# A one-core encoder layer: order of the Gram products, place of the decay's tanh, place of the inverse's products, and order of the first down tile

## The chip, the cores and the metric

The kernel runs on one core of one Trainium2 chip. The metric is the device time of one execution in microseconds (us), the median of several runs. A core has a matrix engine (TensorE, in the profile PE, with PEld for its weight loads), VectorE (DVE), ScalarE (ACT), GpSimd (POOL) and a queue engine (SyncE, SP) that here issues all DMAs. Each engine works through its own list of instructions in a fixed order, and waits on semaphores for the others. SBUF is the on-chip memory, PSUM the small memory into which TensorE writes.

## The reference

One layer of a streaming encoder: sequence 1024, width 1024, batch 1, all in float32. Three groups of heads (64 wide) work side by side: mLSTM (4 heads), retention (6), RWKV-7 (6). Then comes a SwiGLU feed-forward of width 2816 and a last RMSNorm.

```python
h = rmsnorm(x, ln1_g)
pm, pr, pw = split(h @ w_in)
y = concat(mlstm_group(pm), retention_group(pr), rwkv7_group(pw))
x = x + y @ w_out
h = rmsnorm(x, ln2_g)
x = x + (silu(h @ w_gate) * (h @ w_up)) @ w_down
out = rmsnorm(x, lnf_g)
```

The part of RWKV-7 that matters here:

```python
w_log = -softplus(-(w0 + tanh(wl) @ w_up)) - 0.5
decay = exp(-exp(w_log))                     # equals exp(-exp(-0.5) * sigmoid(w0 + ...))
kk = k * k_k, normalised per head;  k = k * (1 + (a - 1) * k_a)
S = S * w_t - (S kk_t)(kk_t * a_t)^T + v_t k_t^T ;  y_t = S r_t      # per frame
```

## The kernel before, in words

**Number form.** Large matrix products are made of three products: each float32 operand is split into a rounded high part (`split_hi`, line 90, ScalarE) and the remainder (`split_lo`, line 93, VectorE), and high x high, high x low and low x high are summed in PSUM. `three` (lines 119 to 121) does it for the projections, lines 740 to 742 for the products laid out by token, `product` (1218 to 1220) for gate and up, `mult` in `down` (1412 to 1414) for down. Their weights come through `w_part` (line 101). These are called dense work below. The mixers' small matmuls take float32 operands directly.

**How the order comes about.** The mixers' work is written as Python generators. `weave` runs them against a planned clock: a generator yields `(cost, delay)`, the clock advances by the cost, and it is called again once the delay is over, or yields the name of an event that another generator signals. `rwkv_proj`, `fillers` and `out_proj` share the dense work, a quarter of a tile at a time (`PART`, 1.38 us). The tile framework then orders each engine's instructions with a scheduler of its own: earlier written goes first, but what it foresees as ready may pass what is not. `tc.issue_after(ins)` forbids this for what is written inside it on the engine of `ins`: it stays behind `ins` in the queue, without waiting for its end. `weave` uses it to keep a generator's TensorE instructions behind the last dense one.

**RWKV-7.** Heads go in three pairs (`i`), the sequence in two halves (`h`), so there are six half-sequences, each of eight chunks of 64 frames. Head `q` (0 even, 1 odd) of a pair lies on partitions `rows_of(q)`, 0 to 63 or 64 to 127. Of one half-sequence:

- `rwkv_half` prepares it. `pa` (line 391) and `pw` (393) are the projections of the rates; `th` (395) is the tanh of the first. Then come `kk` (397), its squares (399), their sums (402), the new keys, the bonus `pb` (412), and the centred values `pt` (421) with their four copies (423 to 426). `cs` (428) is the tanh of the decay, from `pw`; 429 to 431 turn it into running sums, and `er` (434) and `ek` are exponentials of them. Lines 456 to 459 build `kb` and `E`.
- The Gram matrices follow (line 466): for each group of four chunks (`c0`), two PSUM tiles, one for each head; VectorE masks them into `E` (472 to 474). The loop is written chunk by chunk with the two heads in turn, but nothing holds the scheduler to it.
- `rwkv_inverse` solves the unit triangular systems. Their blocks go to DRAM (`ab_d`) and come back rearranged (`MN`, `R`), VectorE solves them (520 to 528), the result goes out (`r_d`, 534) and back into `E` (538). VectorE transposes two blocks (542); TensorE makes the off-diagonal blocks by two sets of 16 small products (547 and 553), with ScalarE copies between (550, 556).
- `rwkv_chain` carries the state through the chunks (588 to 618). It waits for the inverse. The preparation of pair `i`, half `h` begins when the chain of pair `i - 1`, half `h` is done. `rwkv_out` (655) takes the results.

PSUM tiles come from three rings: `acc` (3 buffers), `misc` (3) and `chain` (2). All of the mixers' small products but the chain's use `misc`. Most float32 temporaries of the preparation come from a ring of nine (`tmp`, tag `t`).

**Feed-forward.** `wino` makes gate and up for pairs of 128-row tiles from 7 products each for gate and up (5 for the first pair), items in a list in order. `down(h, d, sl)` makes one output tile from 22 row tiles `f` in six items of up to four (`f0` = 0, 4, ..., 20); an item's weights are prepared three items ahead (`AHEAD`). Its operands are the activations of half `h`: they were stored to `a_dram`, are fetched back by `fetch` into the two `rg` buffers (line 1356), and split by `take`; those of `f` 18 to 21 (`DIRECT`) of the first half are still in SBUF and not fetched. `GROUPS` are `f` 0 to 7, 8 to 15 and 16 to 21. Which `take` comes after which item is written out at the end:

```python
if i == last - 9:
    fetch(0, 0)
if i in (last - 5, last - 4):
    take(0, i - last + 5)
elif i in (last - 1, last + 1):
    take(0, 2, slice((i - last + 1) // 2, (i - last + 1) // 2 + 1))
```

`last` is the index of the first down item. So `f` 0 to 7 are taken at `last - 5`, 8 to 15 at `last - 4`, 16 to 19 at `last - 1`, 20 and 21 at `last + 1`.

Of the kernel before, what the change touches and what calls it, by code (L numbers as in the profile page):

```python
# [11 lines left out]
F32 = mybir.dt.float32  # L12
F32R = mybir.dt.float32r
AF = mybir.ActivationFunctionType
# [5 lines left out]
P = 128  # L20
T = 1024
D = 1024
HF = 512
# [4 lines left out]
FT = D_FF // P  # L28
# [26 lines left out]
def trunk_kernel(ctx: ExitStack, tc: tile.TileContext, a: dict, out: bass.AP):  # L55
# [16 lines left out]
    def misc_tile():  # L72
        return ps_m.tile([P, HF], F32, name="misc", tag="misc")
# [55 lines left out]
    def late(eng):  # L129

        return tc.issue_after(next(i for i in reversed(nc.cur_bb.bb.instructions) if i.engine == eng.engine))
    dense = [None]

    def signal(name, after=0.0):
        events[name] = clock[0] + after
# [40 lines left out]
    two = (0, 1)  # L176
# [12 lines left out]
    def rows_of(q):  # L189
        return slice(q * 64, (q + 1) * 64)  # L190
# [196 lines left out]
    def rwkv_half(i, h, r, k, v):  # L387
# [5 lines left out]
        PE.matmul(pw, lhsT=up[0:64, ch], rhs=wa[h][0:64, :], start=True, stop=True)  # L393
        th = tmp(name="th")
        S.activation(th, pa, AF.Tanh, scale=0.5, bias=ha0[:, i:i + 1])
        kk = tmp(name="kk")
        S.activation(kk, k, AF.Copy, scale=vc("k_k", i))
        t1 = tmp(name="t1")
# [25 lines left out]
        S.copy(out=X[0:64, 0::2, 1, :], in_=p4[0:64, :, 1, :])  # L424
        S.copy(out=X[64:128, 0::2, 0, :], in_=p4[0:64, :, 0, :])
        S.copy(out=X[0:64, 1::2, 1, :], in_=p4[64:128, :, 1, :])
        cs = tmp(name="cs")
        S.activation(cs, pw, AF.Tanh, scale=0.5, bias=hw0[:, i:i + 1])
        V.tensor_scalar(cs, cs, 0.5, 0.5, ALU.mult, ALU.add)
        for z in (slice(z, z + P) for z in range(0, HF, P)):  # L430
            V.tensor_tensor_scan(cs[:, z], data0=cc("reset"), data1=cs[:, z], initial=0.0, op0=ALU.mult, op1=ALU.add)
# [28 lines left out]
        yield 1.2, 7.0  # L460
        for c0 in range(0, 8, 4):
            grams = [misc_tile().rearrange("p (c x) -> p c x", c=4) for _ in two]
            for c in range(4):
                for q, g4 in enumerate(grams):
                    rows = rows_of(q)
                    PE.matmul(g4[:, c, :], lhsT=kb[rows, c0 + c, :, :].rearrange("p a t -> p (a t)"),
                              rhs=E[rows, c0 + c, q, 128:256], start=True, stop=True)
            for q, g4 in enumerate(grams):
                rows, orow = rows_of(q), rows_of(1 - q)
                cs4 = slice(c0, c0 + 4)  # L470
                msk = cc("mask_k").unsqueeze(1).broadcast_to([P, 4, 64])
                V.tensor_tensor(E[orow, cs4, q, 192:256], g4[rows, :, 0:64], msk[rows], ALU.mult)
                V.tensor_tensor(E[orow, cs4, q, 128:192], g4[orow, :, 0:64], msk[orow], ALU.mult)
                V.tensor_tensor(E[:, cs4, q, 64:128], g4[:, :, 64:128],
                                cc("mask_r").unsqueeze(1).broadcast_to([P, 4, 64]), ALU.mult)
# [30 lines left out]
    def rwkv_inverse():  # L506
        for i in range(3):
            for h in range(2):
                yield f"ab{i}{h}"
                E, ab_d = hv_E[i, h]  # L510
                MN = sb.tile([P, 32, 32], F32, name="MN", tag="MN")
                R = sb.tile([P, 8, 32], F32, name="R", tag="R")
                SY.dma_start(out=MN, in_=ab_d.rearrange("b q c s t -> (b q c) (s t)").unsqueeze(0).broadcast_to([4, 32, 1024]))
                SY.dma_start(out=R, in_=ab_d.rearrange("b q c (j g) t -> g (b q c) j t", g=4))
                yield 0.0, 11.0

                mf = MN.rearrange("p s t -> p (s t)")
                tv = ev.tile([P, 516], F32, name="rt", tag="ev")[:, 0:480].rearrange("p (s t) -> p s t", t=32)
                with late(V):
                    V.tensor_tensor(tv, mf[:, 34:34 + 15 * 66:66].unsqueeze(2).broadcast_to([P, 15, 32]), MN[:, 2:31:2], ALU.mult)  # L520
                V.tensor_tensor(MN[:, 1:30:2], MN[:, 1:30:2], tv, ALU.add)
                for u in range(1, 31, 2):
                    n, w = (u + 4) // 4, 31 - u
                    tv = sb.tile([P, 256], F32, name="rt", tag="tq", bufs=2)[:, 0:2 * n * w].rearrange("p (s j t) -> p s j t", j=2, t=w)
                    V.tensor_tensor(tv, R[:, 0:n, u:u + 2].unsqueeze(3).broadcast_to([P, n, 2, w]),
                                    MN[:, u:u + 2, u + 1:32].unsqueeze(1).broadcast_to([P, n, 2, w]), ALU.mult)
                    for j in range(2):
                        V.tensor_tensor(R[:, 0:n, u + 1:32], R[:, 0:n, u + 1:32], tv[:, :, j], ALU.add)
                yield 0.0, INV
                r_d = dram.tile([2, 2, 8, 32, 32], F32, name="r_d", tag=f"r_d{i}{h}")  # L530
                rf = R.rearrange("p s t -> p (s t)")
                for g in range(4):
                    G.memset(rf[lane(g), g::36], 1.0)
                SY.dma_start(out=r_d.rearrange("b q c (j g) t -> g (b q c) j t", g=4), in_=R)
                T11, Q = (sb.tile([P, 8, 32], F32, name="tq", tag="tq", bufs=2) for _ in two)
                for q in range(2):
                    for b in range(2):
                        SY.dma_start(out=E[blk(q, b), :, q, col(b)], in_=r_d[b, q].rearrange("c s t -> s c t"))
                yield 0.0, 9.0
                for q in range(2):  # L540
                    with late(V):
                        V.transpose(out=T11[blk(q, 0)], in_=E[blk(q, 0), :, q, col(0)])
                pqr = misc_tile()
                q3, r3 = (pqr[:, z:z + 256].rearrange("p (c t) -> p c t", c=8) for z in (0, 256))
                for c in range(8):
                    for q in range(2):
                        PE.matmul(q3[blk(q, 1), c, :], lhsT=E[blk(q, 0), c, q, col(1)], rhs=T11[blk(q, 0), c, :],
                                  start=True, stop=True)
                for q in range(2):
                    S.copy(out=Q[blk(q, 1)], in_=q3[blk(q, 1)])  # L550
                for c in range(8):
                    for q in range(2):
                        PE.matmul(r3[blk(q, 0), c, :], lhsT=Q[blk(q, 1), c, :], rhs=E[blk(q, 1), c, q, col(1)],
                                  start=True, stop=True)
                for q in range(2):
                    S.copy(out=E[blk(q, 0), :, q, col(1)], in_=r3[blk(q, 0)])
                signal(f"inv{i}{h}", 2.5)
                yield 1.7, 3.0
# [620 lines left out]
    with ExitStack() as ph3:  # L1179
# [221 lines left out]
        def down(h, d, sl):  # L1401
            box = {}

            def mult(f0, w):
# [27 lines left out]
                if d == KT - 1:  # L1432
# [2 lines left out]
                    ends[0] = final(h, sl, [sqa, sq])  # L1435

            return [(lambda f=f: w_split(w_part(a["w_down"][d][:, f:min(f + 4, FT)])), lambda w, f=f: mult(f, w))
                    for f in range(0, FT, 4)]

        ends = [iter(())]  # L1440
        pairs = [wino(j, m) for j in range(FT // 2) for m in two]
# [62 lines left out]
        for i in range(len(items) + AHEAD):  # L1504
# [6 lines left out]
            ready[i] = None  # L1511
            if i == last - 9:
                fetch(0, 0)
            if i in (last - 5, last - 4):
                take(0, i - last + 5)
            elif i in (last - 1, last + 1):
                take(0, 2, slice((i - last + 1) // 2, (i - last + 1) // 2 + 1))
            if i == last - 1:
                for h in two:
                    x3[h] = big.tile([P, KT, HF], F32, name="x3", tag="E")  # L1520
# [96 lines left out]
```

## Time and profile before

| what | value |
|---|---|
| median of 3 runs | 1493.16 us (1493.12 to 1493.8) |
| profiled execution: its own time | 1485.33 us |
| profiled execution: span from first to last instruction | 1483.5 us |
| mean granted TensorE clock | 0.969 |
| busy share: TensorE, VectorE, ScalarE, GpSimd | 95%, 60%, 37%, 29% |
| mixers and first half's output, 0 to 735 us | TensorE 682.91 us busy, clock 0.95 |
| gate and up, 800 to 1223 us | TensorE 422.92 us busy, clock 1.00 |
| first down tile, 1223 to 1240 us | TensorE 12.57 us busy, clock 0.90 |

Busy times are unions over an engine's instructions. The granted clock is what the chip's throttle allowed TensorE, as a share of full speed. A row of the timeline gives start, length (both us), engine, line and operation, output and inputs, count, and in brackets the idle time of the engine before it and what ended it. A row of windows gives start and end of the stretch, its length, the busy time of each engine with its number of instructions, the granted clock, and the share and rate of the DMA engines. A row under a line's own view names whom the engine waited for, the total in us and how many times. Float32 matmuls stand as two instructions each, and each has a weight load.

### The profile page before, as it was taken

How to read it: one execution, taken by the hardware profiler on the slowest of the kernel's cores; microseconds unless marked ns; L12 is line 12 of the kernel's file. 1: busy time of each engine (PE TensorE's matmuls, PEld its weight loads, DVE VectorE, ACT ScalarE, POOL GpSimd, SP SyncE). 2: the span in 40 equal slices, each digit the busy share in tenths (PEclk: the TensorE clock that was granted, in tenths of full speed). 3: DMA queues.
4: the chain of work that ended last, by engine and by line, in shares of the span. 5: the costliest groups of instructions: out<-in, count | busy, mean ns of one | idle time of the engine just before them, and what ended most of it. 6: DMA issues, size and time to landing. Idle time of an engine off the chain costs nothing.

```text
span 1483.5 us, 23145 instructions
## 1 busy us (share of the span) xinstructions
PE 1410.4 (95%) x8450; PEld 1145.0 (77%) x8450; DVE 890.6 (60%) x1760; ACT 545.2 (37%) x1179; POOL 436.5 (29%) x539
## 2 busy tenths in 40 slices
PE   7998998989999999999998999999999999999997
PEld 5777777887767888887776887888888877888886
DVE  7457585676766757755587555555555574347434
ACT  7352344323223243344545332233333354224222
POOL 3211022335433232334374444443333420000000
PEclk9998999979997999999999999999999999999998
DMA  5132232344431344463542222222222138337333
GB/s 203 51 132 66 67 98 77 81 116 125 126 85 56 100 123 141 121 196 109 178 160 72 76 86 86 85 86 85 86 86 79 52 137 285 97 96 240 98 97 117
DMA packets 131461, 165.33 MB, mean 111 GB/s; under 512 B 44532, under 2 KB 80532, under 8 KB 130196
## 3 DMA queue, kind: packets, MB, share of 16 engines
q1 hardware_dynamic: 131348, 163.87, 34.9%
q8 instruction: 66, 1.08, 0.3%
q14 instruction: 47, 0.39, 0.1%
HBM read 126.06 MB, written 37.77 MB: 110 GB/s over the span
## 4 chain that ended last, share of the span: by engine, by line
PE 70%; DVE 7%; DMA 5%; issue 5%; ACT 3%; POOL 3%; SPq 1%; DVEq 0%; POOLq 0%; ACTq 0%
PE acc L1218 5%; PE acc L1219 5%; PE acc L1220 5%; PE chain L1414 5%; PE chain L1413 5%; PE chain L1412 5%; PE acc L119 4%; PE misc L1219 4%; PE misc L1220 4%; PE misc L1218 4%; PE acc L121 4%; PE acc L120 3%; PE acc L740 2%; PE acc L741 2%; PE acc L742 2%
## 5 line engine op out<-in xcount | busy, mean ns | idle before, releaser
L93 DVE TENSOR_TENSOR wlo<-wraw,whi 128x512 fp32r<-128x512 f32 (+1 forms) x210 | 150.0, 719 | 128.1 <-ACT whi L90 124.6
L90 ACT ACTIVATE whi<-wraw 128x512 fp32r<-128x512 f32 (+1 forms) x210 | 128.2, 613 | 239.7 <-PE chain L1413 124.5
L90 ACT ACTIVATE whi<-rg 128x512 fp32r<-128x512 f32 x128 | 79.8, 631 | 226.6 <-POOL rg L1279 89.3
L93 DVE TENSOR_TENSOR wlo<-rg,whi 128x512 fp32r<-128x512 f32 x128 | 93.0, 727 | 107.9 <-ACT whi L90 107.9
L740 PE MATMUL acc<-whi,act 128*128 128x256 f32 (+1 forms) x512 | 154.2, 306 | 3.3 <-ACT whi L90 2.6
L119 PE MATMUL acc<-act,whi 128*128 128x512 f32 x352 | 149.6, 425 | 6.8 <-ACT whi L90 6.2
L741 PE MATMUL acc<-wlo,act 128*128 128x256 f32 (+1 forms) x512 | 151.3, 296 | 3.4 <-DVE wlo L93 3.3
L742 PE MATMUL acc<-whi,act 128*128 128x256 f32 (+1 forms) x512 | 149.8, 293 | 0.0
L1412 PE MATMUL chain<-act,whi 128*128 128x512 f32 (+1 forms) x374 | 143.6, 384 | 3.7 <-ACT act L90 3.7
L121 PE MATMUL acc<-act,wlo 128*128 128x512 f32 x352 | 144.3, 410 | 2.3 <-DVE wlo L93 2.3
L120 PE MATMUL acc<-act,whi 128*128 128x512 f32 x352 | 143.4, 407 | 1.8 <-DVE act L258 1.8
L1413 PE MATMUL chain<-act,whi 128*128 128x512 f32 (+1 forms) x374 | 142.9, 382 | 0.8 <-DVE act L93 0.8
L1414 PE MATMUL chain<-act,wlo 128*128 128x512 f32 (+1 forms) x374 | 143.2, 383 | 0.0
L1220 PE MATMUL acc<-act,wlo 128*128 128x512 f32 x352 | 139.7, 397 | 3.5 <-DVE wlo L93 3.5
L1218 PE MATMUL acc<-act,whi 128*128 128x512 f32 x352 | 140.2, 398 | 2.1 <-ACT whi L90 1.1
L1219 PE MATMUL acc<-act,whi 128*128 128x512 f32 x352 | 139.2, 396 | 0.0
L740 PEld LDWEIGHTS acc<-whi,act 128*128 128x128 f32 x512 | 100.0, 197 | 9.3 <-ACT whi L90 3.4
L741 PEld LDWEIGHTS acc<-wlo,act 128*128 128x128 f32 x512 | 100.9, 197 | 7.9 <-DVE wlo L93 4.4
L1219 PE MATMUL misc<-act,whi 128*128 128x512 f32 x264 | 104.0, 394 | 0.0
L1220 PE MATMUL misc<-act,wlo 128*128 128x512 f32 x264 | 104.0, 394 | 0.0
L1218 PE MATMUL misc<-act,whi 128*128 128x512 f32 x264 | 104.0, 394 | 0.0
L742 PEld LDWEIGHTS acc<-whi,act 128*128 128x128 f32 x512 | 100.6, 197 | 1.5 <-issue 0.3
(328 smaller groups left out, 2822.2 us busy)
## 6 DMA issues: line engine op xcount, KB each, us to landing
wraw<-in_w_down SPq DMA_DIRECT2D x85, 256.0 KB
rg<-in_w_gate SPq DMA_DIRECT2D x22, 512.0 KB
rg<-in_w_up SPq DMA_DIRECT2D x22, 512.0 KB
wraw<-in_w_tm SPq DMA_DIRECT2D x40, 256.0 KB
a_dram<-work SPq DMA_DIRECT2D x39, 256.0 KB
rg<-a_dram SPq DMA_DIRECT2D x9, 1024.0 KB
v_dram<-vt SPq DMA_DIRECT2D x64, 128.0 KB
wraw<-in_w_out SPq DMA_DIRECT2D x32, 256.0 KB
```

What stands on the lines that cost most here:

```text
L90: S.activation(hi, src, AF.Copy, scale=scale)
L93: (eng or V).tensor_tensor(lo, src, hi.bitcast(F32), ALU.subtract)
L119: PE.matmul(ps, lhsT=hi, rhs=xh[:, k, :], start=(k == 0), stop=False)
L740: PE.matmul(o, lhsT=xh[h][:, k, sl], rhs=w[k][0], start=(k == 0), stop=False)
L741: PE.matmul(o, lhsT=xh[h][:, k, sl], rhs=w[k][1], start=False, stop=False)
L742: dense[0] = PE.matmul(o, lhsT=xl[h][:, k, sl], rhs=w[k][0], start=False, stop=(k == KT - 1)).ins
L1218: PE.matmul(ps, lhsT=hi, rhs=hi_x[:, k, :], start=(start and k == 0), stop=False, skip_group_check=True)
L1219: PE.matmul(ps, lhsT=hi, rhs=lo_x[:, k, :], start=False, stop=False, skip_group_check=True)
L1220: PE.matmul(ps, lhsT=lo, rhs=hi_x[:, k, :], start=False, stop=(stop and k == 3), skip_group_check=True)
L1412: PE.matmul(ps, lhsT=hi, rhs=hi_a[:, sl], start=(f == 0), stop=False)
L1413: PE.matmul(ps, lhsT=hi, rhs=lo_a[:, sl], start=False, stop=False)
L1414: PE.matmul(ps, lhsT=lo, rhs=hi_a[:, sl], start=False, stop=(f == FT - 1))
```

## The change

Four edits:

1. The Gram products are issued through a new helper, `alternate`: the products of the two heads for one chunk form a pair, and each pair is issued after the last product of the pair before.
2. The decay's tanh (`cs`) is written right after `th`, before `kk`, and gets a tile with a tag of its own instead of one from the ring of nine.
3. In `rwkv_inverse` a yield with a delay of 1.5 us stands between VectorE's transposes and the products.
4. The first down tile (first half, `d` = 0) takes its items in the order `f` = 0, 4, 8, 16, 12, 20. The `take` calls change with it: 0 to 7 at `last - 5`, 8 to 11 at `last - 4`, 16 to 19 at `last - 1`, 12 to 15 at `last`, 20 and 21 at `last + 1`.

```diff
+    def alternate(*rows):
+        prev = None
+        for pair in zip(*rows):
+            with nullcontext() if prev is None else tc.issue_after(prev):
+                for mm in pair:
+                    prev = mm().ins
...
         th = tmp(name="th")
         S.activation(th, pa, AF.Tanh, scale=0.5, bias=ha0[:, i:i + 1])
+        cs = sb.tile([P, HF], F32, name="cs", tag="cs")
+        S.activation(cs, pw, AF.Tanh, scale=0.5, bias=hw0[:, i:i + 1])
...
-        cs = tmp(name="cs")
-        S.activation(cs, pw, AF.Tanh, scale=0.5, bias=hw0[:, i:i + 1])
         V.tensor_scalar(cs, cs, 0.5, 0.5, ALU.mult, ALU.add)
...
-            for c in range(4):
-                for q, g4 in enumerate(grams):
-                    rows = rows_of(q)
-                    PE.matmul(g4[:, c, :], lhsT=kb[rows, c0 + c, :, :].rearrange("p a t -> p (a t)"),
-                              rhs=E[rows, c0 + c, q, 128:256], start=True, stop=True)
+            gram = lambda q, c: PE.matmul(grams[q][:, c, :], lhsT=kb[rows_of(q), c0 + c, :, :].rearrange("p a t -> p (a t)"),
+                                          rhs=E[rows_of(q), c0 + c, q, 128:256], start=True, stop=True)
+            alternate(*([lambda q=q, c=c: gram(q, c) for c in range(4)] for q in two))
...
                     with late(V):
                         V.transpose(out=T11[blk(q, 0)], in_=E[blk(q, 0), :, q, col(0)])
+                yield 0.0, 1.5
                 pqr = misc_tile()
...
-                    for f in range(0, FT, 4)]
+                    for f in ((0, 4, 8, 16, 12, 20) if (h, d) == (0, 0) else range(0, FT, 4))]
...
-            if i in (last - 5, last - 4):
-                take(0, i - last + 5)
-            elif i in (last - 1, last + 1):
-                take(0, 2, slice((i - last + 1) // 2, (i - last + 1) // 2 + 1))
+            for n, (g, z) in {last - 5: (0, 0), last - 4: (1, 0), last - 1: (2, 0), last: (1, 1), last + 1: (2, 1)}.items():
+                if i == n:
+                    take(0, g, slice(z, z + 1) if g else None)
```

## The prediction

> **What bounds the kernel now.** I read the page first (shares, slices, granted clock), then busy time by stage, then the idle time of TensorE, then the stretches after each longer idle time, because the page shows a clock under full speed in only some slices.
>
> ```profile
> span 1483.5 us, 23145 instructions
> PE 1410.4 (95%) x8450; PEld 1145.0 (77%) x8450; DVE 890.6 (60%) x1760; ACT 545.2 (37%) x1179; POOL 436.5 (29%) x539
> PEclk9998999979997999999999999999999999999998
> ```
>
> TensorE is busy for 95% of the span; no other engine comes near. By stages (start, length, then busy time of PE, PEld, DVE, ACT, POOL, and the granted clock):
>
> ```profile
> core 0: us, PE busy (x) PEld busy (x) DVE busy (x) ACT busy (x) POOL busy (x), PEclk, DMA share, GB/s
> 0.00:735.00 735.00, 682.91 (x5245) 555.53 (x5246) 478.15 (x1193) 283.56 (x744) 231.97 (x398) 0.95 0.37 111
> 800.00:1223.00 423.00, 422.92 (x1821) 341.50 (x1819) 235.47 (x321) 143.87 (x246) 162.52 (x113) 1.00 0.24 85
> 1223.00:1240.00 17.00, 12.57 (x47) 9.86 (x47) 10.32 (x16) 6.93 (x10) 0.00 (x0) 0.90 0.78 270
> ```
>
> The gate and up products (800 to 1223) are full at full clock; nothing is to be had there. The mixers (0 to 735) hold 52 us of idle TensorE and run at 0.95 of the clock, and the first down tile (1223 to 1240) has 4.4 us idle at 0.90. All four edits fall in these two places. The lost clock is concentrated (same columns):
>
> ```profile
> 136.06:142.90 6.84, 6.75 (x19) 5.58 (x20) 5.04 (x19) 0.00 (x0) 0.10 (x1) 0.50 0.13 24
> 439.84:460.30 20.46, 20.46 (x131) 12.61 (x129) 6.13 (x13) 6.62 (x16) 4.55 (x6) 0.50 0.08 23
> 1228.30:1231.70 3.40, 3.40 (x9) 2.61 (x8) 3.09 (x4) 1.66 (x2) 0.00 (x0) 0.50 0.85 324
> ```
>
> In each the clock is 0.50. Each follows an idle time of TensorE (1.61, 2.62 and 3.66 us; the rows come below). So an idle time costs itself and up to half of the half-rate stretch behind it.
>
> **Gram matrices in turns.** The edit removes and adds no matmul. Now the scheduler may take all of one head's products first; after it, each pair (q=0, q=1) must follow the pair before. All Gram matmuls by window (busy time of PE and of PEld, then clock, DMA share, GB/s):
>
> ```profile
> 95.50:97.60 2.10, 1.97 (x16) 1.78 (x16) 1.00 0.99 369
> 131.10:133.20 2.10, 2.05 (x24) 1.86 (x24) 1.00 0.74 232
> 274.60:275.80 1.20, 1.11 (x8) 0.96 (x8) 1.00 0.06 14
> 481.40:482.60 1.20, 1.13 (x8) 0.96 (x8) 1.00 0.45 149
> sum 24.90, PE 21.68 PEld 18.91; mean PE 1.97 PEld 1.72
> ```
>
> Sixteen take 1.97 us and eight 1.11, so one more costs (1.97 - 1.11) / 8 = 0.11 us where one head follows the other. Yet 24 take only 2.05 us: eight singles of 0.11 leave 1.17 us for the other 16. I read these as pairs of heads, which use different halves of the array's rows and run at once. The six half-sequences have 32 each, two groups of 16 apiece: in pairs 12 x 1.17 = 14.0 us against 21.68, or 7.7 us less. What may take that back is the wait of the second group:
>
> ```profile
>   DVE E L474: 1.8, 2
>   DVE R L528: 1.6, 1
>   DVE E L458: 0.6, 1
> 136.15 1.19 PE L466 MATMUL misc<-E,kb 64*128 64x128 f32 x4 [1.61 <-DVE R L528]
> 481.43 1.13 PE L466 MATMUL misc<-E,kb 64*128 64x128 f32 x8 [1.49 <-DVE E L474]
> ```
>
> A group takes two of three `misc` PSUM tiles, so the second group's q=1 products wait for VectorE to empty one (L474 is its last read). Before, q=0's eight ran meanwhile; now they queue behind q=1's first, and VectorE gets their result later, all six masking steps together. Other work must cover: the dense products, which the scheduler puts there as far as it foresees the wait. Three second groups wait today (1.61, 1.49 and, of the 1.8 on L474, 0.3 us; L528 is the step beside L474 in VectorE's queue). There I take the eight moved singles, 0.88 us, as lost cover: 3 x 0.88 = 2.6. The term is -7.7 + 2.6 = **-5.1 us**. Its ends are -7.7 and +2.1: the singles were cover in all six (5.3 back), and three more waits like that at 481.43 come (4.5).
>
> ```profile
> L472 DVE TENSOR_TENSOR E<-misc,cst 64x256 f32<-64x256 f32 x24 | 10.1, 422 | 6.9 <-PE misc L466 6.2
> ```
>
> Emptying is the longer side: 72 such steps (24 each at L472, L473, L474; this row, 10.1 us for 24) are 30 us, 5.0 per half-sequence, against 2.3 for paired products. [...] I keep -5.1.
>
> **The inverse's products later.** Only one of the six inverses shows idle TensorE before L547:
>
> ```profile
> 437.32 1.81 SPq L538 DMA_DIRECT2D E<-r_d  x4
> 436.63 0.40 PE L120 MATMUL acc<-act,whi 128*128 128x512 f32 x1
> 439.65 0.24 PE L547 MATMUL misc<-tq,E 32*32 32x32 f32 x2 [2.62 <-DVE tq L542]
> ```
>
> The solved blocks come back by DMA (issued from 437.32), VectorE transposes them, and the products stand in TensorE's queue ahead of dense matmuls that could have run. The new step of 1.5 us lets the planner place one dense part (six matmuls, 0.23 us from start to start as in the down rows below, 1.4 us) first. That leaves 2.62 - 1.4 = 1.2 us idle. The 1.61 us at 136.15 were followed by half rate, the 1.49 at 481.43 were not (1.00 in its window above), so at 1.2 I expect full rate. Full rate for 20.46 us is worth at most 10.2 us; I take 4.6, a bit less than half, because prep matmuls in that stretch feed on ScalarE and VectorE (6.6 and 6.1 us busy), whose pace does not change. Term: -1.4 - 4.6 = **-6.0 us**, ends -12.8 (gap and all of the clock) and +4.2. The upper end is the price if cover is gone: every inverse ends 1.4 us later, its copies on ScalarE and then the state recurrence wait for it, and three half-sequences stand in series at the end of the mixers, 3 x 1.4. There the cover is thin already:
>
> ```profile
> 729.84 0.68 PE L655 MATMUL misc<-cst,yw 64*64 64x64 f32 x16 [1.46 <-POOL yw L853]
> ```
>
> I take zero for it, since the first output tile of the second half can run seven of its eight k-steps before that.
>
> **Decay's tanh at once.** The same 0.69 us activation moves ahead of the scaled keys and their squares on ScalarE, into a tile of its own instead of one of nine shared ones (its readers of the half-sequence before are long done); its PSUM tile comes free sooner.
>
> ```profile
> 446.44 0.63 ACT L399 ACTIVATE t<-kk 128x512 f32<-128x512 f32 x1
> 465.38 0.69 ACT L428 ACTIVATE cs<-misc,hw 128x512 f32<-128x512 f32 x1
>   ACT cs L428: 4.9, 3
>   ACT t L399: 4.0, 6
> ```
>
> In three half-sequences the tanh runs late and VectorE waits for it, 4.9 us in all (third row, of L429). On TensorE that is worth only the 0.6 us above (E L458). Against it, the norm's matmuls (L402) already wait for the squares (fourth row, L399); where the tanh is moved ahead of them they wait 0.69 us more, 3 x 0.69 = 2.1. Term: 2.1 - 0.6 = **+1.5 us**; ends -4.9 and +4.1 (six times 0.69).
>
> **Down's first tile.** Before, `f` runs 0, 4, 8, 12, 16, 20, and TensorE stops at 12:
>
> ```profile
> 1218.08 0.36 SPq L1356 DMA_DIRECT2D rg<-a_dram  x1
> 1221.05 0.41 SPq L1356 DMA_DIRECT2D rg<-a_dram  x1
> 1225.61 2.00 ACT L90 ACTIVATE act<-rg 128x1024 fp32r<-128x1024 f32 x2 [2.54 <-DMA rg<-a_dram]
> 1228.27 1.06 ACT L90 ACTIVATE act<-rg 128x1024 fp32r<-128x1024 f32 x1 [0.66 <-DMA rg<-a_dram]
> 1222.42 0.40 PE L1413 MATMUL chain<-act,whi 128*128 128x512 f32 x1
> 1222.66 0.40 PE L1414 MATMUL chain<-act,wlo 128*128 128x512 f32 x1
> 1226.72 0.50 PE L1412 MATMUL chain<-act,whi 128*128 128x512 f32 x1 [3.66 <-ACT act L90]
> 1227.97 0.52 PE L1413 MATMUL chain<-act,whi 128*128 128x512 f32 x1 [0.76 <-DVE act L93]
> 1236.57 0.69 DVE L1423 TENSOR_TENSOR dn<-chain,RS 128x512 f32<-128x512 f32 x1 [3.06 <-PE chain L1414]
> ```
>
> On SP's queue the fetch of 16, 17 (half the bytes; 18 to 21 are taken from SBUF) now stands before that of 12 to 15. The second fetch landed 2.66 us after the first, so I estimate: 16 lands at 1225.61 - 2.66 = 1222.95, and 12, with the same bytes in sum, at 1228.27. TensorE follows 1.11 us after a landing and its second matmul 1.25 later. Group 16 then runs from 1224.06 to 1227.9 (1.25 and eleven steps of 0.23), group 12 from 1229.38 to 1233.2, and 20 and 21 (six steps) end at 1234.6, where VectorE's L1423 took over at 1236.57. The stall becomes two, of 1.0 and 1.5 us: what is late next is fetch 12. Term **-2.0 us**, ends -6.1 (3.66, 0.76 and half of 3.4 gone) and +1.4 (3.4 us at half rate after both). The weights follow the new order on the same queue, at no cost, as they come three items ahead.
>
> **Sum.** -5.1 - 6.0 + 1.5 - 2.0 = -11.6 us. The profiled execution took 1485.33 us (span 1483.5, 1.8 around it), which would become 1473.7; it is 7.8 us under the median of the timed runs, 1493.16, so the comparable figure is 1493.16 - 11.6 = **1481.6 us**.
>
> **The rivals.** (a) *The half rate after the inverse stays.* The stretch at 439.84 is six times the one that followed 3.66 us idle, so the gap may not be its only cause. Then the inverse brings 1.4 and the total is 1486. [...] (b) *Emptying PSUM eats the pairing*: Gram term 0, total 1486.7. (c) *The savings come back as waits*: the recurrence and the DMA round trips of the inverse set the pace, as the 1.46 us at 729.84 hints, and TensorE's free time turns idle: within 3 us of 1493. Against it: only 52 of 735 us are idle. (d) *Slower: each half-sequence's second Gram group stalls as the one at 136.15 does.* There 1.61 us idle and 6.84 us at half rate cost 1.6 + 3.4 = 5.0 us. Holding q=0's eight behind q=1 takes away what now bridges that wait in the other five. From three such stalls on (11.6 lost, 15 paid) the kernel is slower by over 3 us; four give 1481.6 + 20 = 1501.6. For it: the waits on L474. Against: dense work is ready nearly everywhere in the mixers.
>
> **How the numbers follow.** The forecast as summed 0.42; (a) 0.18; (b) 0.08; (c) 0.12; (d) 0.20. Faster: 0.42 + 0.18 + 0.08 = 0.68; same 0.12; slower 0.20. About 0.2%, 3 us, is what a measurement of this kernel tells from no change. The likeliest case alone spans 1473 to 1488 (half the bounds of its terms). The range 1470 to 1501 takes in all cases but the deepest sum of gains (0.06) and (d) with four stalls or more (0.12).
>
> **What would show it.** Gram windows of 16 in about 1.2 us and some 14 us in sum; no idle time over 1.3 us before L547 and no 20 us at half rate behind it; L428 within 2 us of L395; in down's first tile two short waits, and L1423 some 2 us nearer to the last gate and up product. The prediction is wrong if second Gram groups show waits of 1.5 us or more with 0.50 clock behind them, or if the mixers' idle time grows by what their busy time falls: the orders of all engines are made anew by the scheduler, and one new stall like that at 439.65 costs 2.62 + 10.2 us.

## The result and the profile after

The changed kernel takes 1497.68 us (median; 1492.76 to 1512.47), the kernel before 1491.18 us in the same comparison (1482.2 to 1493.8): ratio 1.0056, 95% interval 1.0038 to 1.0075. (The ratio is not that of the two medians, which is 1.0044.) The forecast was a gain of 11.6 us; by the medians the change costs 6.5. The profiled execution of after took 1496.41 us. One run of one experiment below, e_vmem_inv, was over 1.5% slower than the fastest of its kernel and is left out of its row.

The head of its page (busy time and share of each engine, then the granted clock by slices):

```profile
span 1494.4 us, 23139 instructions
PE 1406.6 (94%) x8450; PEld 1145.9 (77%) x8450; DVE 888.7 (59%) x1760; ACT 544.2 (36%) x1179; POOL 430.8 (29%) x539
PEclk9999999979999997899999999999999999999999
```

TensorE is busy 3.8 us less than before and the span is 10.9 us longer, so the work did not grow: waiting did. By stages, in the windows that the prediction used (start and end, length, then busy time of PE, PEld, DVE, ACT and POOL, clock, DMA share, GB/s):

```profile
0.00:735.00 735.00, 666.97 (x5159) 547.67 (x5160) 469.07 (x1176) 273.78 (x721) 220.57 (x392) 0.93 0.36 107
800.00:1223.00 423.00, 422.11 (x1822) 341.46 (x1821) 236.78 (x325) 145.13 (x249) 165.70 (x115) 1.00 0.23 78
1223.00:1240.00 17.00, 15.56 (x65) 11.82 (x64) 13.67 (x16) 9.77 (x14) 3.78 (x2) 1.00 0.75 275
```

In the mixers idle time rises from 52.1 to 68.0 us, and the clock falls from 0.95 to 0.93; the last window, where down begins, is better than before in both. Two marks in the timeline (start, length, engine, line, idle before) say the same:

```profile
745.68 0.51 PE L662 MATMUL misc<-cst,yw 64*64 64x64 f32 x10 [0.66 <-POOL yw L860]
1249.00 0.68 DVE L1430 TENSOR_TENSOR dn<-chain,RS 128x512 f32<-128x512 f32 x1
```

The last group of `rwkv_out` starts at 745.68 instead of 729.84, 15.8 us later; down's first result is read at 1249.00 instead of 1236.57, only 12.4 later. So everything lost is lost before 746, and 3.4 us come back after it. Where the mixers wait, the lines of the products by token show (line, form, count, then busy time, mean ns, and idle time before them with its releasers), and then the rows of the four longest waits behind the first product:

```profile
L747 PE MATMUL acc<-whi,act 128*128 128x256 f32 (+1 forms) x512 | 159.0, 313 | 15.4 <-ACT whi L90 15.4
505.23 0.58 PE L747 MATMUL acc<-whi,act 128*128 128x256 f32 x1 [6.94 <-ACT whi L90]
613.02 0.80 PE L747 MATMUL acc<-whi,act 128*128 128x256 f32 x2 [6.32 <-ACT whi L90]
259.88 1.22 PE L422 MATMUL misc<-t,cst 128*128 128x512 f32 x1 [5.72 <-DVE t L420]
408.75 0.28 PE L928 MATMUL misc<-MV,mks 128*64 128x65 f32 x2 [3.93 <-DVE mks L922]
```

Two new stalls, of 6.9 and 6.3 us, wait for a split weight (`whi`); neither stands at a line that the diff touches. Around them the clock is halved (start and end, length, busy times, clock):

```profile
501.96:508.79 6.83, 3.56 (x27) 3.34 (x27) 5.29 (x11) 0.63 (x1) 3.25 (x4) 0.50 0.42 141
611.19:621.43 10.24, 8.41 (x48) 7.28 (x49) 6.75 (x20) 2.90 (x8) 4.77 (x5) 0.50 0.30 107
```

That is 13.3 us idle and 12.0 us of work at half rate, some 19 us, where the stall that the step was to remove had cost 12.8 at most (2.62 and half of 20.46). Not all of it is new: the kernel before has half rate near both places too, 3.4 us from 501.3 and 6.8 us from 600.3.

How the stall at 505 comes about can be followed through four queues (SPq is the instruction that issues a transfer; its length is the time for which SP stood in it):

```profile
490.11 0.55 SPq L520 DMA_DIRECT2D R<-ab_d  x1
492.90 6.72 SPq L778 DMA_DIRECT2D v_dram<-vt  x1
499.66 1.40 SPq L101 DMA_DIRECT2D wraw<-in_w_tm  x3
501.06 0.10 POOL L539 MEMSET R<- 32x8 f32 x1 [8.19 <-DMA R<-ab_d]
503.47 1.04 POOL L737 TENSOR_TENSOR wraw<-wraw,wmean 128x512 f32<-128x512 f32 x1 [1.59 <-DVE wmean L736]
504.54 0.63 ACT L90 ACTIVATE whi<-wraw 128x512 fp32r<-128x512 f32 x1 [7.93 <-POOL wraw L737]
```

SP issues the transfer of `R`, the systems that VectorE is to solve; the transfer behind it holds SP for 6.72 us, and three weight loads (`wraw`) stand behind that. On GpSimd the setting of R's diagonal waits 8.19 us for the same transfer, ahead of the weights' centring (L737). Then the weight is split, and TensorE goes on. In the kernel before there is the same transfer and the same 7 us on SP, behind it:

```profile
489.10 0.53 SPq L514 DMA_DIRECT2D R<-ab_d  x1
491.34 7.11 SPq L738 DMA_DIRECT2D rot<-in_rot  x1
```

There a small table (`rot`) stood in that place, the weight loads came later, from 502.46 on, and the longest wait of TensorE nearby is 1.47 us. The stall at 613 in after has the same form: three weight loads behind R's transfer take SP 9.81 us from 597.98 on, and GpSimd waits 12.21 us, until 608.34. So the question for the experiments is which part of the change put the weights there.

### The profile page after: what moved, and what is told of

Read it like the earlier page. It is cut to its first block, busy times and chain, and to the rows that moved or that the text cites. A ratio compares the mean times of both kernels' runs of the same rounds, so it can differ in the third digit from the quotient of the medians.

```text
span 1494.4 us, 23139 instructions
## 1 busy us (share of the span) xinstructions
PE 1406.6 (94%) x8450; PEld 1145.9 (77%) x8450; DVE 888.7 (59%) x1760; ACT 544.2 (36%) x1179; POOL 430.8 (29%) x539
## 4 chain that ended last, share of the span: by engine, by line
PE 55%; DVE 4%; DMA 4%; issue 2%; ACT 2%; POOL 1%; SPq 1%; POOLq 0%; DVEq 0%; ACTq 0%
PE acc L1225 5%; PE acc L1227 5%; PE acc L1226 5%; PE chain L1419 5%; PE chain L1421 5%; PE chain L1420 5%; PE misc L1227 4%; PE misc L1226 4%; PE misc L1225 4%; DMA wraw<-in_w_tm 1%; PE acc L119 1%; PE acc L120 1%; PE acc L747 1%; PE acc L121 1%; DVE wlo L93 1%
## 5 line engine op out<-in xcount | busy, mean ns | idle before, releaser
L93 DVE TENSOR_TENSOR wlo<-wraw,whi 128x512 fp32r<-128x512 f32 (+1 forms) x210 | 149.7, 720 | 132.3 <-ACT whi L90 127.0
L747 PE MATMUL acc<-whi,act 128*128 128x256 f32 (+1 forms) x512 | 159.0, 313 | 15.4 <-ACT whi L90 15.4
L93 DVE TENSOR_TENSOR wlo<-rg,whi 128x512 fp32r<-128x512 f32 x128 | 93.0, 727 | 107.3 <-ACT whi L90 107.2
L749 PE MATMUL acc<-whi,act 128*128 128x256 f32 (+1 forms) x512 | 152.9, 300 | 0.0
L747 PEld LDWEIGHTS acc<-whi,act 128*128 128x128 f32 x512 | 102.9, 202 | 21.6 <-ACT whi L90 16.2
L749 PEld LDWEIGHTS acc<-whi,act 128*128 128x128 f32 x512 | 104.1, 204 | 1.6 <-issue 0.8
```

Source lines behind the costliest of these rows:

```text
L93: (eng or V).tensor_tensor(lo, src, hi.bitcast(F32), ALU.subtract)
L747: PE.matmul(o, lhsT=xh[h][:, k, sl], rhs=w[k][0], start=(k == 0), stop=False)
L749: dense[0] = PE.matmul(o, lhsT=xl[h][:, k, sl], rhs=w[k][0], start=False, stop=(k == KT - 1)).ins
```

## The experiments

In the table, "full rate" is the median over the timed runs of span x granted clock, and "lost" is the rest of the span. The granted clock is a mean over the whole span, idle time included: half of any idle time that falls into a half-rate stretch counts as lost, too. So the two columns do not part clock from waiting; the profiles do. The kernel before has 1438 to 1439 and 49 to 51 in each group of runs.

| run | what | median us | ratio, 95% interval | full rate | lost |
|---|---|---|---|---|---|
| after | the change | 1497.7 | 1.0056 [1.0038, 1.0075] | 1438.5 | 56.8 |
| e_gram | Gram in turns alone | 1490.3 | 0.9996 [0.9972, 1.0020] | 1441.4 | 46.2 |
| e_tanh | early tanh alone | 1481.0 | 0.9937 [0.9910, 0.9964] | 1436.4 | 43.6 |
| e_inv | step of 1.5 us alone | 1505.8 | 1.0112 [1.0067, 1.0157] | 1439.5 | 63.9 |
| e_down | down's order alone | 1488.7 | 0.9988 [0.9958, 1.0018] | 1438.4 | 49.1 |
| e_no_inv | the change without the step | 1477.6 | 0.9929 [0.9899, 0.9959] | 1431.5 | 44.3 |
| e_tanh_tile | tanh late, own tile | 1489.7 | 1.0003 [0.9977, 1.0029] | 1436.1 | 51.3 |
| e_plan15 | 1.5 us in the planned solve | 1490.1 | 0.9997 [0.9971, 1.0022] | 1442.5 | 46.0 |
| e_inv30 | step of 3.0 us alone | 1484.8 | 0.9979 [0.9955, 1.0003] | 1433.2 | 48.9 |
| e_vmem_inv | e_inv, R's diagonal on VectorE | 1511.3 | 1.0138 [1.0092, 1.0185] | 1437.1 | 72.5 |
| e_actq_inv | e_inv, MN and R sent by ScalarE | 1531.5 | 1.0276 [1.0246, 1.0306] | 1447.5 | 82.6 |
| e_actq_no_inv | e_no_inv, the same | 1496.8 | 1.0040 [1.0012, 1.0068] | 1440.9 | 52.3 |
| e_actq_vmem_inv | e_inv, both | 1528.4 | 1.0272 [1.0234, 1.0310] | 1443.4 | 82.5 |
| e_pin | old turns, products later | 1491.4 | 1.0016 [0.9992, 1.0041] | 1438.0 | 52.2 |
| e_order | new turns, products not later | 1507.3 | 1.0127 [1.0096, 1.0158] | 1442.6 | 65.5 |
| e_pin_all | the change, turns of e_no_inv | 1474.3 | 0.9901 [0.9870, 0.9933] | 1431.2 | 42.7 |

### Which part it is

**Each part alone.** Each edit was put into the kernel before by itself, and the step was taken out of the whole change: `yield 0.0, 1.5` is the whole of it.

> The kernel before with the Gram products in turns alone. Theory A (the pairing saves what was summed, and the loss of the full change comes from new waits that the re-made order brings): TensorE's Gram windows fall from 21.7 us in sum to about 14, the mixers' work at full rate by 7 to 9 us; the second groups wait no longer than before (at most 2 us each), and the time lies 3 to 8 us under before unless a new stall of 5 us or more stands somewhere in the mixers. Rival R1 (the pairing itself causes the loss, each second group stalls TensorE): three or more idle times of 1.5 us or more stand right before Gram products, and the time is 5 to 15 us over before.

> The kernel before with the decay's tanh early and in its own tile alone. Theory A: little on its own, -5 to +4 us as forecast. Rival R2 (the early tanh is the cause: VectorE then takes the decay's four scans ahead of the bonus' operand, so the bonus product L412's successor waits): the idle time of TensorE before the bonus product grows from 3.7 us in sum to about 11 as in the full change, and the time is 5 to 10 us over before.

> The kernel before with the 1.5 us step before the inverse's products alone. Theory A: no idle time over 1.3 us right before the products (2.6 before), but the order of all queues is re-made; -6 us as forecast if no new stall comes, +5 or more if stalls like the two of 6 to 7 us in the full change (TensorE waiting for weights behind GpSimd) are already there. Rival R3 (later products lengthen the recurrence, which sets the pace): the last output of the recurrence moves by 3 to 5 us or more with TensorE idle just before it, and no stall over 5 us elsewhere.

> The kernel before with down's first tile in the new order alone. All theories: the mixers unchanged, the time from the first down product to the emptying of the first tile falls from 22.0 to about 20 us, the half-rate stretch of 3.4 us behind the 3.66 us wait goes, total -2 us (0 to -4).

> The full change without the 1.5 us step before the inverse's products. So far the step alone cost 16 us (ratio 1.011), the early tanh alone brought 9 us (0.994), the Gram pairs and the down order alone nothing clear. Theory A (the step is the cause of the loss, through the new order of the queues): under before by 5 to 14 us. Rival R4 (the edits work against each other, the parts are not additive): within 3 us of before or over it.

The step alone costs 1.12%, the others nothing that can be told or -0.63%; the four add up to 0.33% against 0.56% measured, which is additive within the intervals (0.2 to 0.5% to each side). The change without the step is faster than both kernels. The step's cost is waiting and clock together: from before to e_inv, the idle time of TensorE in the profile goes from 73.1 to 86.8 us, and its busy time in half-rate stretches from 77.6 to 94.0 us, half of which is loss; counted so, its work falls by 6.5 us, and the three add up to the difference of the two spans. The row of e_inv that answers to after's 505.23, and the longest of e_gram:

```profile
508.54 0.58 PE L741 MATMUL acc<-whi,act 128*128 128x256 f32 x1 [7.88 <-ACT whi L90]
```

```profile
408.85 0.58 PE L898 MATMUL misc<-mq 64*128 64x128 f32 x2 [8.32 <-DMA mq<-mqk_dram]
```

**Is it the delay as such?** A rival, called R3 in the expectations, is that the later products lengthen the recurrence. It was tried by the size of the delay and by its place: 3.0 instead of 1.5 us, and 1.5 us added to the planned time of the solve (`INV` 28.0 to 29.5).

```diff
                         V.transpose(out=T11[blk(q, 0)], in_=E[blk(q, 0), :, q, col(0)])
+                yield 0.0, 3.0
                 pqr = misc_tile()
```

> The kernel before with a step of 3.0 us, twice as long, before the inverse's products. Theory A: no proportion between step and cost; anywhere from -10 to +17 us. Rival R3: about twice the loss of 1.5 us, +25 to +35 us.

> The kernel before with the same 1.5 us put into the planned time of the inverse's solving on VectorE (28.0 to 29.5 us), so before the result's transfers and not before the products. Theory A (what costs is the re-made order, not the place of the products): the time may lie anywhere from -10 to +17 us, with stalls in other places than with the step. Rival R3 (every planned microsecond in the inverse lengthens the recurrence): +12 to +20 us, as with the step, the last output of the recurrence near 745 us.

Twice the delay costs nothing (0.9979), and the same 1.5 us planned one step earlier neither (0.9997). A longer recurrence would grow with the delay; R3 does not fit. Yet e_inv30 has the same stall:

```profile
501.46 0.58 PE L741 MATMUL acc<-whi,act 128*128 128x256 f32 x1 [7.40 <-ACT whi L90]
```

So this one stall doesn't settle a version's total.

### What holds the weights

**GpSimd's wait, then SP's.** Two explanations of the stall near 505: GpSimd's diagonal of `R` (theory A1, e_vmem_inv), or SP's queue behind R's transfer (A2, e_actq_inv and e_actq_no_inv).

```diff
-                    G.memset(rf[lane(g), g::36], 1.0)
+                    V.memset(rf[lane(g), g::36], 1.0)          # e_vmem_inv, inside late(V)
-                SY.dma_start(out=MN, ...); SY.dma_start(out=R, ...)
+                S.dma_start(out=MN, ...); S.dma_start(out=R, ...)   # e_actq_*
```

> The kernel before with the 1.5 us step, and the four memsets that put ones on the diagonal of R moved from GpSimd, where they stand early and wait for R's transfer, to VectorE behind its last solving step. Theory A1 (the stalls of 7.9 us at 508.5 and 3.9 us at 611.8 come from this wait of GpSimd: a value tile stands behind it, the tile's store holds SP's queue, and weight loads stand behind the store): GpSimd's waits of 8 us on R's transfer are gone, the two stalls are under 2 us each, and the time falls by 10 to 18 us against the step alone, to about 1488 to 1495. Rival R5 (the stalls come from the transfers being late, whatever stands behind GpSimd): stalls stay within 2 us of their size.

> The kernel before with the 1.5 us step, and the two transfers that bring the inverse's blocks back (MN and R) issued by ScalarE instead of SP. In every trace so far the first transfer that SP issues after R's takes 4 to 10 us instead of 0.3 in every half-sequence, whatever it is. Theory A2 (the stalls of 7.9 and 3.9 us come from this block: in the order that the step makes, weight loads stand right behind it): no transfer of SP takes over 3 us behind R's, the two stalls before the split of weights are under 2 us each, and the time falls by 10 to 18 us against the step alone, to about 1488 to 1495. Rival R6 (the block is shared by the DMA engines, not SP's): SP's transfers still take 4 to 10 us there, no gain. Rival R7 (the stalls are only a part of the loss): the stalls go, but the time stays over 1497.

> The full change without the 1.5 us step (1477.6 us measured), with MN and R issued by ScalarE. Theory A2: SP's blocked time of 4 to 10 us per half-sequence is gone; the three waits for weights of 1.1 to 1.6 us between 490 and 532 us shrink; 2 to 8 us under 1477.6. Rival R6 or R7: no gain, or a loss where ScalarE's list now waits for the blocks' way to DRAM.

With the diagonal on VectorE the stall stayed, since SP still stood before the loads; A1 falls.

```profile
493.78 5.69 SPq L773 DMA_DIRECT2D v_dram<-vt  x1
499.52 1.40 SPq L101 DMA_DIRECT2D wraw<-in_w_tm  x3
506.41 0.58 PE L742 MATMUL acc<-whi,act 128*128 128x256 f32 x1 [8.19 <-ACT whi L90]
```

With `MN` and `R` sent by ScalarE SP's longest instruction falls from 9.8 us in e_inv to 2.3 in e_actq_inv; there the transfer at 510.58 takes 0.32 us and the two weight loads behind it 0.94. But the weight loads were issued only from 511.14 on, and the stall stayed: GpSimd waited until 521.41. A2 alone falls. The total gets worse, with the step and without it: e_actq_no_inv is at 1.0040 where e_no_inv is at 0.9929.

```profile
511.14 0.94 SPq L101 DMA_DIRECT2D wraw<-in_w_tm  x2
521.41 0.10 POOL L533 MEMSET R<- 32x8 f32 x1 [8.72 <-DMA R<-ab_d]
523.94 0.58 PE L741 MATMUL acc<-whi,act 128*128 128x256 f32 x1 [7.29 <-ACT whi L90]
```

**Both at once** (A3: two locks in series).

> The step of 1.5 us with MN's and R's transfers issued by ScalarE and R's diagonal set by VectorE: neither SP's queue nor GpSimd stands behind R's transfer any more. Theory A3 (two locks in series make the stall near 505 us, each enough alone): the stall at 500 to 525 us with the split of the weights falls under 2.5 us; the total stays at 1505 to 1530 us since ScalarE's own waits remain (with one lock gone they made 1531 us). Rival: a stall of over 5 us stays there, so neither lock was its cause, and the order of the weight loads themselves is.

The stall is 5.7 us still, so A3 falls as well. The DMA share (last but one column) tells a part of why:

```profile
514.00:516.00 2.00, 2.00 (x23) 1.80 (x24) 1.76 (x5) 0.21 (x1) 1.90 (x3) 1.00 0.87 220
516.00:518.00 2.00, 2.00 (x23) 1.93 (x22) 0.00 (x0) 0.41 (x2) 0.34 (x1) 1.00 1.05 178
518.00:520.00 2.00, 1.18 (x10) 0.98 (x9) 0.00 (x0) 0.00 (x0) 0.00 (x0) 1.00 0.59 146
520.00:522.00 2.00, 0.00 (x0) 0.00 (x0) 0.00 (x0) 0.00 (x0) 0.00 (x0) 0.97 0.26 89
522.12 0.69 DVE L730 TENSOR_REDUCE wmean<-wraw 128x8 f32<-128x512 f32 x1 [6.37 <-DMA wraw<-in_w_tm]
524.90 0.58 PE L742 MATMUL acc<-whi,act 128*128 128x256 f32 x1 [5.72 <-ACT whi L90]
```

The weights were issued at 513.67 and not used before 522.12. From 514 to 518 the DMA engines' share was 0.87 and 1.05; from 518 to 522, when TensorE ran out of work, it was 0.59 and 0.26. So what held the load to the end stays open. A weight load that the order puts beside R's transfer came late in each of these kernels, with either lock gone and with both (TensorE waits for the split weight 7.88 us in e_inv, 8.19 in e_vmem_inv, 7.29 in e_actq_inv, 5.72 in e_actq_vmem_inv). Not every load there hurts: in the kernel before one is held behind R's transfer for 10.7 us at 283.7, and no product of L740 to L742 waits over 1.5 us in that trace. That leaves the order, which load stands there and how soon it is needed, as the cause by exclusion; the next runs test it.

### The products or the turns

The step does two things: it puts the products some steps later, and, since `weave` deals each turn by its clock, it deals all later turns anew. To part the two, `weave` was made to read its turns from a list, recorded from another version.

```diff
-            ready = [...]; clock[0] = max(...); s = next(s for s, r in zip(live, ready) if r <= clock[0])
+            s = every[turn]          # for turn in ORDER
```

- e_pin: turns of the kernel before, the products moved by as many steps as in e_inv.
- e_order: turns of e_inv, the products at once.
- e_pin_all: the whole change with the turns of e_no_inv, the products moved.

(The turns of the kernel before and of e_no_inv are the same list, those of e_inv and of after too.) With before's list and no edit each engine's order is that of the kernel before, instruction for instruction. Of the 721 places in SP's order of transfers, 41 differ between e_pin and before, 257 between e_inv and before, 16 between e_order and e_inv (by the tile written and its source, in the traces).

> The kernel before with the inverse's products put two or three steps later (the places that the step of 1.5 us gives them), while all other steps of the mixers keep the turns that they have in the kernel before: the turns are read from a list instead of from the planner's clock. Theory O (the step's own effect is small and the slowdown of 1.1% comes from the turns that the planner deals anew to everything behind the first step): within 0.4% of before, 1484 to 1494 us, no stall of over 5 us with a weight split behind R near 500 us. Rival R3 (the products' delay itself lengthens the recurrence): slower by 0.6% or more, 1498 us and up. My forecast on record for the step (-6 us): 1483 us.

> The other half: the turns that the planner deals with the step of 1.5 us, read from a list, but the inverse's products issued at once with their transposes, as in the kernel before. Theory O: as slow as the step, 1500 to 1510 us (ratio 1.008 to 1.014), with the stall of 7 to 8 us near 505 us. Rival R3: the slowdown goes with the delay, 1485 to 1493 us.

> The whole change, the products put later included, with all other steps in the turns of the version without the step. Theory O: near the version without the step, 1473 to 1484 us (ratio 0.989 to 0.996), where the change as given is at 1.0056. Rival R3: the step's slowdown stays, 1493 us or more.

The turns carry the loss; which of the stalls that they make costs how much is not shown. With the new turns and the products in their old place the kernel is as slow as e_inv (1.0127 against 1.0112), with the same stall:

```profile
498.86 5.68 SPq L768 DMA_DIRECT2D v_dram<-vt  x1
504.59 1.40 SPq L110 DMA_DIRECT2D wraw<-in_w_tm  x3
511.12 0.58 PE L737 MATMUL acc<-whi,act 128*128 128x256 f32 x1 [7.82 <-ACT whi L99]
```

With the old turns and the products later it isn't slower (1.0016, 0.9992 to 1.0041), and the whole change in old turns takes 1474.3 us, 0.9901: the lowest median here, though its interval overlaps that of e_no_inv. In e_pin no stall of over 2 us waits for a weight in the products by token. But it didn't gain the forecast 6 us either:

```profile
389.72 9.27 SPq L769 DMA_DIRECT2D v_dram<-vt  x1
399.04 0.93 SPq L110 DMA_DIRECT2D wraw<-in_w_cm  x2
403.08 0.63 ACT L99 ACTIVATE whi<-wraw 128x512 fp32r<-128x512 f32 x1 [13.47 <-DMA wraw<-in_w_cm]
406.01 0.48 PE L591 MATMUL chain<-pm,E 64*64 64x64 f32 x4 [10.05 <-ACT pm L588]
447.78 0.69 PE L545 MATMUL misc<-tq,E 32*32 32x32 f32 x32
```

The inverse's products (last row) start without idle time now, and the half rate behind them is gone. But at 399 two weight loads stand behind R's transfer of that half-sequence, ScalarE waits 13.47 us for them, and the recurrence's copy (`pm`) is queued behind that: 10.05 us idle at 406. In the kernel before ScalarE makes that copy ahead of the split, and the longest wait nearby is 3.33 us at 400.68, for another transfer. The tile framework's own scheduler still moves a few instructions when the products move; that these few make the new stall is read from the rows and was not tested.

### The early tanh

e_tanh_tile keeps the tanh in its old place and gives it the tile of its own.

> The kernel before with the decay's tanh at its old place, but in a tile of its own. The early tanh with its own tile brought 9 us. Theory A (the gain is the order that came about: the 20 us at half rate behind the wait before the inverse's products at 439.65 is gone, no part of it needs the early place): anywhere from -10 to +5 us. Rival R8 (it is the early place: VectorE gets the decay sooner): within 3 us of before, with the late tanh and its wait on VectorE (4.9 us) as before.

The tile alone does nothing (1.0003), so the gain of 0.63% in e_tanh needs the early place. In e_tanh the inverse's products find their transposes done, without the step:

```profile
441.31 0.22 PE L547 MATMUL misc<-tq,E 32*32 32x32 f32 x2
```

The 2.62 us and the 20.46 us at half rate of the kernel before are gone there, and TensorE's busy time in half-rate stretches falls from 77.6 to 64.5 us. VectorE does not wait less for `cs`: 4.9 us in before, 12.2 in e_tanh, 13.5 in e_tanh_tile. That this stall carries all of the gain is not shown: in e_no_inv it is back, with 2.28 us, and that kernel is faster still.

## Why the prediction was wrong, point by point

**The inverse's step: the step of the prediction that failed.** Term -6.0, ends -12.8 and +4.2; measured +16.7 us alone (1.0112 of 1489.77). In the place of the edit the stall went, as forecast. Rows of after:

```profile
448.45 0.24 PE L554 MATMUL misc<-tq,E 32*32 32x32 f32 x2
449.29 0.69 PE L554 MATMUL misc<-tq,E 32*32 32x32 f32 x30
```

No idle time before L554, and full rate behind it (clock 1.00 up to 464.4). (In after the new turns alone would do that: e_order, with the products at once, has no idle time there either. With the old turns it is e_pin that shows it, at 447.78.) The prediction costed the edit in its own place, plus the recurrence behind it. It named what would make it wrong, idle time that grows by what busy time falls since all orders are made anew, and gave the price of one such stall, but no term and no chance in the sum. That was the whole loss: e_order has it without the delay, e_pin_all has the delay without it. And with the turns held the forecast gain of 6 us stayed away as well (e_pin, 1.0016), beside a new stall of 10.05 us. In the profile of after idle time grows by nearly twice what work falls by: in the mixers up to the last group of `rwkv_out`, TensorE's work (busy time, half rate counted half) falls by 8.6 us, idle time rises by 16.6, and half rate takes 7.9 more, together the 15.8 us.

**Gram in turns: mechanism right, the gain not kept.** Windows over all Gram products of after: the two rows of one half-sequence at full rate, one row at half rate, and the sum:

```profile
133.80:135.20 1.40, 1.36 (x18) 1.19 (x18) 1.00 0.86 293
139.00:140.15 1.15, 1.12 (x14) 0.96 (x14) 1.00 0.04 16
585.00:587.20 2.20, 2.08 (x16) 1.79 (x16) 0.50 0.00 0
sum 19.00, PE 17.79 PEld 14.89; mean PE 1.19 PEld 0.99
```

Thirty-two products take 2.5 us where 12 x 1.17 for six half-sequences had been forecast, 2.3 each; the sum is 17.8 against 21.7, the last half-sequence being at half rate. So some 4 us of the 7.7 came off TensorE (4.9 in e_gram, where the sum is 16.9). The cover that was to be lost at the second groups wasn't: their waits are 0.8 us in all on the masking and once 1.8 beside the solve, no more than before. But alone the edit changes the time by -0.04% (-0.28 to +0.20%): the work saved came back as waits elsewhere, as in e_gram's 8.32 us before L898; TensorE is idle for 84.8 us in its profile against 73.1 in before. That is rival (c), for this one term.

**Tanh: mis-sized, and with the wrong sign.** +1.5 forecast, ends -4.9 and +4.1; -9.4 us measured (-0.63%), outside both ends. The forecast looked at who waits for the tanh and for the squares. The runs show that the gain needs the early place and that the inverse's stall does not arise in e_tanh; that the one is the reason of the other is not shown.

**Down's first tile: right in sum, and only where the clock stayed up.** Forecast -2.0, and two short stalls. After, and then e_down at half rate:

```profile
1238.09 0.50 PE L1419 MATMUL chain<-act,whi 128*128 128x512 f32 x1 [0.51 <-ACT act L90]
1239.35 0.49 PE L1420 MATMUL chain<-act,whi 128*128 128x512 f32 x1 [0.76 <-DVE act L93]
1226.00:1229.40 3.40, 3.40 (x9) 2.65 (x9) 1.51 (x3) 0.84 (x1) 0.00 (x0) 0.50 0.83 308
```

From the first down product to the first eviction 19.93 us instead of 22.02 in after: -2.1, and the half rate at 1228 is gone. The stalls lie otherwise than forecast: some 2 us at the fourth item, the fetch of 16 (the two rows and 0.71 us at 1240.55), instead of 1.0, and next to none at the fetch of 12 instead of 1.5. In e_down alone the stall at the fetch of 16 is about as long, but 3.4 us at half rate stand behind it, and the same stretch takes 21.70 us: -0.3. So that the term came out in after is in part luck with the clock. In the total of e_down, -0.12%, it can't be told from nothing.

**The rivals.** (a), half rate staying after the inverse: no, that stretch is gone. (b), PSUM's emptying: not seen, the pairs run at 1.36 for 18 between waits that did not grow. (c), the savings come back as waits: true of the Gram term, and of the step with the turns held. (d), second Gram groups that stall: one does, with 1.76 us at 139.03 and half rate behind it, as one did before (1.61 us at 136.15); no others. The slower outcome, with a chance of 0.20, came by a mechanism that none of the rivals had. That 1497.7 us lies between 1470 and 1501 is luck: that end of the range was there for (d).

**The clock.** The prediction took the lost clock for concentrated. The three stretches that it shows are 30.7 us; the kernel before has eight more at 0.50, 81.7 us in all without the end of the span. It also expected full rate from the length of the idle time, 1.2 us against 1.61 and 1.49. That length doesn't decide: in before, 1.47 us idle at 501.48 come with half rate (501.30 to 504.70), and in after half rate comes behind 3.40 us in which TensorE was busy throughout by the profile:

```profile
358.60:362.00 3.40, 3.40 (x31) 2.86 (x30) 2.43 (x6) 1.55 (x6) 3.34 (x6) 1.00 0.13 41
362.00:365.40 3.40, 3.40 (x22) 3.06 (x21) 2.37 (x7) 0.12 (x1) 1.48 (x4) 0.50 0.21 56
```

In the clock records of before and after each half-rate stretch but the last lasts 3.41 us or a whole multiple of it (6.83, 10.24, 13.65, 17.07, 20.48). What brings the clock down here stays open. The pace of ScalarE and VectorE did not change with it, as the prediction took it: in before L399 takes 0.63 us at half rate (446.44) and 0.63 in the mean of the five at full rate, and L93 on 128x512 0.68 and 0.69 in the median.

## What to carry to other kernels

Where an order is planned by a clock, an edit to a planned time is two edits: a local one, which a profile can price, and a new deal of every later turn, which it can't; part them by replaying the recorded turns, and keep the turns that were good (here 1474.3 us against 1497.7 with the same four edits). Before such a change, look for transfers that block a queue for long (here the one behind R's, 3.3 to 10.7 us), and ask what the new order will put behind them. In this kernel many stalls add up to the idle time, and a gain of 5 us in one place need not show in the total (e_gram): look at the place, and at the others.

## What the runs showed of the hardware that was not expected

- The instruction on SP's queue behind the transfer of `R` holds SP for 5.7 to 9.3 us in the rows above (3.3 to 10.7 in the twelve half-sequences of before and after), whatever it is (`rot`, `v_dram`, a weight load), against a median of 0.33 us for SP's other transfers in those two traces. `MN`, four times as large (512 KB against 128), is issued ahead of `R`, and no run parts the two. When ScalarE issues both (e_actq_vmem_inv), SP's two weight loads at 513.67 take 0.94 us together, and the DMA engines' share is still 0.87 and 1.05 in the 4 us from 514 on.
- Half rate came without idle time of TensorE: in after it is busy for all of the 3.40 us from 358.60 at a clock of 1.00, and from 362.00 the clock is 0.50.
- Between runs of one kernel span and granted clock move together: after at 1491.1 us span had 0.967 and at 1510.5 us 0.953, with the same order of instructions, and span x clock differs by 0.2% between them. Between versions that product hides waiting: e_inv and before have 1439.5 and 1438.4, and differ by 13.7 us in idle time in their profiles.
